# Storing the small inverses of an RWKV-7 recurrence from GpSimd's queue, and two of its last operations on VectorE

## The chip, the core and the metric

The kernel runs on one core of a Trainium2 chip. The metric is the device time of one execution in microseconds (us), lower is better. Engines are named as in the profile: PE is TensorE (matrix products), DVE is VectorE, ACT is ScalarE, POOL is GpSimd, and SP is SyncE, which here does nothing but start transfers. SPq, ACTq and POOLq are the transfer instructions that stand in the instruction stream of SP, ACT and POOL.

## The reference, cut to what matters

One decoder layer over 2048 tokens (plus 16 meta tokens) and 1024 channels: a combined input projection, a sliding-window attention, an RWKV-7 recurrence in parallel with it, a gated merge, an output projection and a SwiGLU network.

```python
proj = u @ w_in[layer] + b_in[layer]
y_attn = sliding_window_sink_attention(q, k, v, attn_sinks[layer])
y_rwkv = rwkv7_time_mix(p_rwkv, ...)
merged = gates[..., :D] * (y_attn @ w_br_attn) + gates[..., D:] * (y_rwkv @ w_br_rwkv)
h = h + merged @ w_o[layer]
h = h + (silu(f @ w_ffn_gate) * (f @ w_ffn_up)) @ w_ffn_down
...
# the recurrence, per head, step by step in time
S = S * w_t + (S @ a_t) b_t + v_t k_t ;  y = S @ r_t
# and its end: group norm of y, then
y = y * ln_w + ln_b
y = y + sum(r * k * r_k) * v          # the bonus
return y * g                          # the output gate
```

## The kernel before

The dense products (input projection `pi`, gated branches `pb`, output projection `ph_o`, network `pg`, `pu`, `ph_d`) run on PE in a fixed program order, block after block of 512 tokens: first phase a for four blocks, then phase c for four blocks. Each 128-row piece of a weight is loaded in float32 by SP (`chunk`, line 212, tile `wr_...`, two buffers), and split by ACT into a high part (`wh_...`) and by DVE into a low part (`wl_...`, five buffers for both); PE uses high and low parts in three products.

Between the dense products the recurrence is woven in. It is cut into 33 units: one for the meta tokens and 32 of 256 tokens and one pair of heads (`rwkv(i, j)`, four chunks of 64 tokens each). Every `yield` of a unit is a place where dense work comes between. The order of PE's instructions is pinned to the order in which the program is written (`InOrder`); the other engines' orders come from a scheduler, and each engine works its own list strictly in turn, so an instruction that waits holds everything behind it on that engine.

In each unit sixteen 32 x 32 triangular matrices are inverted on POOL. PE makes them (`pg`), DVE scales them into `g`, SP stores them to DRAM (`lt_d`, line 744) and loads them back so that each partition has one column to solve for (`lt`, line 754). SP also loads the unit matrix into `xv` (line 757). POOL then does 31 pairs of instructions (lines 761 and 763). The result goes back to DRAM (`xt_d`, line 788) and is loaded as blocks into `td` (line 793), from where the chunk steps (`ch`) use it. `xv` has one buffer: the load of the next unit's `xv` (line 757) must wait until the store of line 788 has read this unit's. `td` has one buffer too.

At a unit's end the chunk outputs are gathered by ACT into `yt` (line 836), normalised, transposed by PE (`pyt`), scaled by ACT into `tl` (line 858), and then the bonus `bv` is added and the gate `gs` multiplied (lines 859 and 860). SP stores the result into `y_d` (line 861), which phase c loads (`yl`, line 415; `ya` is its split).

Of the kernel before, what the change touches and what calls it, by code (L numbers as in the profile page):

```python
# [78 lines left out]
def layer(ctx, tc, x, meta, w_in, w_br, w_o, w_gate, w_up, w_down, w2a, a2, g2, vecs, sinks, gfin,  # L79
          consts, rope, out):  # L80
    nc = tc.nc
    V, A, G, S = nc.vector, nc.scalar, nc.gpsimd, nc.sync
# [43 lines left out]
    xt_d = dp.tile([4 * NU + 1, 16, 32, 32], F32, name="xt_d")  # L126
# [9 lines left out]
    def vc(n, j, rows=slice(None)):  # L136
        return vec[rows, _VC[n][0] + j:_VC[n][0] + j + 1]
# [468 lines left out]
    def rwkv(i, j):  # L606
# [3 lines left out]
        m = i is None  # L610
        uid = 4 * NU if m else 4 * i + j
# [68 lines left out]
        if not m:  # L680
# [10 lines left out]
            gs = t1("gs", 3)  # L691
# [15 lines left out]
        if not m:  # L707
# [3 lines left out]
            bv = t1("bv", 3)  # L711
# [44 lines left out]
        xv = mx.tile([P, 4, 32], F32, tag="xv", bufs=1, name=f"xv_{nm}")  # L756
# [28 lines left out]
                    A.activation(vd[hb, q::2, hb], pvt[qb, :, hb], AF.Copy)  # L785
        for _ in range(WAIT_INV):
            yield
        S.dma_start(xt_d[uid].rearrange("m (b c) i -> b m (c i)", c=4), xv.rearrange("p c i -> p (c i)"))
        lo, hi = [slice(64 * h, 64 * h + 32) for h in range(2)], [slice(64 * h + 32, 64 * h + 64) for h in range(2)]
        for h in range(2):  # L790
            for q, r32 in ((0, lo[h]), (1, hi[h])):
# [64 lines left out]
            T.transpose(pyt[:, t * P:(t + 1) * P], yt[:, t], ident)  # L856
        yf = t1("tl", 2)
        A.activation(yf, pyt[:, :TU], AF.Identity, bias=vc("ln_b", j), scale=vc("ln_w", j))
        G.tensor_add(yf, yf, bv)
        G.tensor_mul(yf, yf, gs)  # L860
        S.dma_start(y_d[4 + j][:, i * TU:(i + 1) * TU], yf)


# [152 lines left out]
    def tick():  # L1016

        turn[0] = (turn[0] + 1) % TURNS
        rs = [u for u in units if u[2] == "r"]
        for u in list(units):  # L1020
            if turn[0] != (0 if u[2] == "a" else 1 if len(rs) > 1 and u is rs[0] else 2):
                continue
            u[1] += 1
            if next(u[0], 0) == 0:
                units.remove(u)
        if todo_r and turn[0] == 2:
            i, j = todo_r[0]
            b = (i or 0) // 2
            young = min((u[1] for u in units if u[2] == "r"), default=LAG)
            if young >= LAG - 3 and i not in asked and set(range(6, 9)) <= emitted[b]:  # L1030
                asked.add(i)
                start("l", lora(i), b)
            if young >= LAG and i in loras and set(
                    range(9, 21) if i is None else range(PAIR0 + 3 * j, PAIR0 + 3 * j + 3)) <= emitted[b]:
                todo_r.pop(0)
                start("r", rwkv(i, j), b)
        if todo_a and turn[0] == 0 and not any(u[2] == "a" for u in units):
            ti = todo_a[0]
            b = (ti or 0) // 4
            if set(range(6)) <= emitted[b]:  # L1040
                todo_a.pop(0)
                start("a", attn_meta() if ti is None else attn(ti), b)
# [135 lines left out]
```

## Time and profile before

| | us |
|---|---|
| three runs: lowest, median, highest | 3446.83, 3450.84, 3458.58 |
| the profiled execution's own time | 3451.51 |
| its span from first to last instruction | 3449.7 |
| mean granted TensorE clock, share of full | 0.976 |

The page of the profile gives the busy time of each engine, and the trace behind it can be asked for single instructions. In all rows times are in microseconds unless marked ns, and L788 is line 788 of the kernel. In a list of waits "A <- B" says that A's engine sat idle until B was done. A transfer instruction's duration is that of its start alone, not of the movement of data.

### The profile page before, as it was taken

The page shows a single profiled execution, that of the slowest core. Times are in us where ns is not written, and L with a number is a line of the kernel's source. Part 1 is how long each engine was busy: PE and PEld are TensorE (multiplying, and loading weights), DVE is VectorE, ACT ScalarE, POOL GpSimd, SP SyncE. Part 2 cuts the span into 40 slices and gives each one's busy share as a digit, 9 for nine tenths or more (in the row PEclk, how much of TensorE's full clock was granted, in tenths as well). Part 3 has the DMA queues.
Part 4 walks back from the last instruction along what each step waited for, and adds up shares of the span by engine and source line. Part 5 has one row for each costly group of instructions (what it writes and reads, how often), then busy time and mean ns, then how long its engine had stood idle before and what let it go on. Part 6 is the DMA issues. An engine that isn't in the chain of part 4 may idle for free.

```text
span 3449.7 us, 47536 instructions
## 1 busy us (share of the span) xinstructions
PE 3285.1 (95%) x16909; PEld 2696.2 (78%) x16909; DVE 1906.8 (55%) x3796; ACT 1499.4 (43%) x3101; POOL 1026.7 (30%) x2321
## 2 busy tenths in 40 slices
PE   8999999999999999999989999999889999999999
PEld 6887777877778777777877788877777888778887
DVE  3344435544444775656666655656665655764555
ACT  4455446555544454445443534434353333432222
POOL 0133333343333344333343334434333332100000
PEclk9999999999999999999999999999999999999999
DMA  4454444454544433333344333324433332532222
GB/s 143 157 145 132 152 127 137 138 154 129 164 129 138 140 103 96 95 96 95 89 142 143 95 94 101 94 85 145 148 94 90 96 91 91 191 98 98 98 97 99
DMA packets 229932, 409.49 MB, mean 119 GB/s; under 512 B 61037, under 2 KB 124013, under 8 KB 229694
## 3 DMA queue, kind: packets, MB, share of 16 engines
q1 hardware_dynamic: 197342, 359.14, 34.4%
q10 hardware_dynamic: 32352, 47.31, 3.9%
q8 instruction: 133, 2.18, 0.3%
q14 instruction: 105, 0.86, 0.1%
HBM read 346.29 MB, written 60.04 MB: 118 GB/s over the span
## 4 chain that ended last, share of the span: by engine, by line
PE 45%; POOL 15%; DMA 7%; issue 7%; DVE 3%; ACT 2%; SPq 1%; POOLq 0%; ACTq 0%; DVEq 0%
PE pg L93 10%; PE pu L93 9%; PE ph_d L93 8%; POOL xv L763 7%; POOL pr L761 7%; PE pi L93 5%; PE pb L93 3%; PE ch L93 2%; DMA lt<-lt_d 2%; PE ph_o L93 2%; PE py L93 1%; DMA lt_d<-g 1%; PE pq L93 1%; DVE h L202 1%; POOL tl L860 1%
## 5 line engine op out<-in xcount | busy, mean ns | idle before, releaser
L93 PE MATMUL pi<-act_u,wh_in 128*128 128x512 f32 x2368 | 765.5, 404 | 2.2 <-DVE act_u L202 2.0
L761 POOL TENSOR_TENSOR pr<-xv,lt 128x124 f32<-128x124 f32 (+30 forms) x992 | 377.6, 381 | 568.2 <-DMA lt<-lt_d 245.4
L93 PEld LDWEIGHTS pi<-act_u,wh_in 128*128 128x128 f32 x2368 | 426.2, 190 | 83.5 <-issue 5.8
L93 PE MATMUL pi<-act_u,wl_in 128*128 128x512 f32 x1184 | 466.8, 394 | 0.4 <-DVE wl_in L202 0.4
L93 PE MATMUL pg<-act_f,wh_g 128*128 128x512 f32 x1408 | 455.0, 404 | 7.0 <-DVE act_f L202 7.0
L93 PE MATMUL pu<-act_f,wh_u 128*128 128x512 f32 x1408 | 449.5, 401 | 0.0
L93 PE MATMUL ph_d<-wh_d,mg_g 128*128 128x512 f32 x1280 | 430.5, 401 | 12.7 <-DVE th L202 10.7
L763 POOL TENSOR_TENSOR xv<-xv,pr 128x124 f32<-128x124 f32 (+30 forms) x992 | 396.5, 400 | 74.2
L93 PEld LDWEIGHTS pg<-act_f,wh_g 128*128 128x128 f32 x1408 | 257.3, 191 | 57.6 <-DVE act_f L202 9.9
L93 PEld LDWEIGHTS pu<-act_f,wh_u 128*128 128x128 f32 x1408 | 259.1, 190 | 50.3 <-issue 1.5
L93 PEld LDWEIGHTS ph_d<-wh_d,mg_g 128*128 128x128 f32 x1280 | 243.3, 190 | 66.3 <-DVE th L202 12.5
L202 DVE TENSOR_TENSOR wl_in<-wr_in,wh_in 128x1024 fp32r<-128x1024 f32 x148 | 186.3, 1259 | 195.7 <-PE pi L93 126.2
L93 PE MATMUL pg<-act_f,wl_g 128*128 128x512 f32 x704 | 278.0, 395 | 0.0
L93 PE MATMUL pu<-act_f,wl_u 128*128 128x512 f32 x704 | 277.1, 394 | 0.0
L93 PEld LDWEIGHTS pi<-act_u,wl_in 128*128 128x128 f32 x1184 | 223.8, 189 | 51.1 <-DVE wl_in L202 0.8
L93 PE MATMUL ph_d<-wl_d,mg_g 128*128 128x512 f32 x640 | 251.9, 394 | 0.0
L850 POOL TENSOR_TENSOR gst<-gst,mhalf 128x4 f32<-128x4 f32 x32 | 35.8, 1119 | 707.5 <-DVE gst L849 610.1
L202 DVE SCALAR_TENSOR_TENSOR h<-ph_d,h 128x512 f32<-128x512 f32 x320 | 216.8, 686 | 52.2 <-PE ph_d L93 51.1
L202 ACT ACTIVATE wh_g<-wr_g 128x1024 fp32r<-128x1024 f32 x88 | 93.3, 1060 | 223.4 <-PE pu L93 72.5
L202 ACT ACTIVATE wh_in<-wr_in 128x1024 fp32r<-128x1024 f32 x148 | 155.8, 1053 | 79.4 <-DMA wr_in<-in_w_in 70.8
L202 DVE TENSOR_TENSOR wl_u<-wr_u,wh_u 128x1024 fp32r<-128x1024 f32 x88 | 109.4, 1243 | 120.4 <-issue 53.9
L202 DVE TENSOR_TENSOR wl_d<-wr_d,wh_d 128x1024 fp32r<-128x1024 f32 x80 | 100.0, 1250 | 129.3 <-PE pg L93 51.2
(356 smaller groups left out, 5965.5 us busy)
## 6 DMA issues: line engine op xcount, KB each, us to landing
wr_in<-in_w_in SPq DMA_DIRECT2D x148, 512.0 KB
wr_g<-in_w_gate SPq DMA_DIRECT2D x88, 512.0 KB
wr_u<-in_w_up SPq DMA_DIRECT2D x88, 512.0 KB
wr_d<-in_w_down SPq DMA_DIRECT2D x80, 512.0 KB
proj_d<-po ACTq DMA_DIRECT2D x84, 256.0 KB
gate_d<-po ACTq DMA_DIRECT2D x64, 256.0 KB
lt<-lt_d SPq DMA_DIRECT2D x32, 512.0 KB
wr_br<-in_w_br SPq DMA_DIRECT2D x32, 512.0 KB
```

Of the source, the lines that this page charges most:

```text
L93: r = f(*p, **k)
L202: return f(*p, **k)
L761: G.tensor_mul(pr[:, :, :n_], xv[:, :, r:r + 1].to_broadcast([P, 4, n_]), lt[:, r, r + 1:].unsqueeze(1).to_broadcast([P, 4, n_]))
L763: G.tensor_add(xv[:, :, r + 1:], xv[:, :, r + 1:], pr[:, :, :n_])
L850: G.tensor_tensor(st[:, 3], st[:, 2], mhalf[:, 0:4], op=ALU.pow)
L860: G.tensor_mul(yf, yf, gs)
```

## The change

The store of each unit's inverses is started by POOL and not by SP, and lines 859 and 860 run on DVE and not on POOL. Nothing else is edited.

```diff
         for _ in range(WAIT_INV):
             yield
-        S.dma_start(xt_d[uid].rearrange("m (b c) i -> b m (c i)", c=4), xv.rearrange("p c i -> p (c i)"))
+        G.dma_start(xt_d[uid].rearrange("m (b c) i -> b m (c i)", c=4), xv.rearrange("p c i -> p (c i)"))
...
         yf = t1("tl", 2)
         A.activation(yf, pyt[:, :TU], AF.Identity, bias=vc("ln_b", j), scale=vc("ln_w", j))
-        G.tensor_add(yf, yf, bv)
-        G.tensor_mul(yf, yf, gs)
+        V.tensor_add(yf, yf, bv)
+        V.tensor_mul(yf, yf, gs)
         S.dma_start(y_d[4 + j][:, i * TU:(i + 1) * TU], yf)
```

The scheduler makes new orders from it. PE's order stays the same. On SP all 33 stores of line 788 are gone. The other transfers keep their order but for seven that moved by one to four places; six of these are loads of the next unit's `xv`, which moved ahead. Three places follow.

SP, around the store of the unit whose inverses are done at 2246.9 us in the trace before (`wr_u` and `wr_g` are weights of the SwiGLU network, `xv_3` is this unit's tile and `xv_0` the next one's):

```order
 L559 DMA rp_1_22717<-proj_d 128x3x257
 L212 DMA wr_g_16_22120<-in_w_gate 128x1024
-L788 DMA xt_d<-xv_3_21635 8x16x128
 L757 DMA xv_0_22373<-in_consts 128x128
 L212 DMA wr_u_16_22193<-in_w_up 128x1024
```

The store left SP's list, and the next unit's `xv` load now follows the load of `wr_g_16` directly. On POOL the same store stands right behind the unit's last addition, ahead of the power of a group norm (line 850) and of the next inverse:

```order
 L761 TENSOR_TENSOR pr_3_30_21727<-xv_3_21635,lt_3_21633 128x4
 L763 TENSOR_TENSOR xv_3_21635<-xv_3_21635,pr_3_30_21727 128x4
+L788 DMA xt_d<-xv_3_21635 8x16x128
 L850 TENSOR_TENSOR gst_2_22274<-gst_2_22274,mhalf 128x4
 L761 TENSOR_TENSOR pr_0_0_22375<-xv_0_22373,lt_0_22371 128x4x31
```

It is the only instruction that POOL gains in a unit.

SP, around the store of the unit whose inverses are done at 2096.6 us (`xv_1` this unit's, `xv_2` the next one's):

```order
 L559 DMA rp_3_21274<-proj_d 128x3x257
 L212 DMA wr_g_9_20654<-in_w_gate 128x1024
-L788 DMA xt_d<-xv_1_20229 8x16x128
+L757 DMA xv_2_20935<-in_consts 128x128
 L212 DMA wr_u_9_20728<-in_w_up 128x1024
-L757 DMA xv_2_20935<-in_consts 128x128
 L212 DMA wr_d_9_0_20777<-in_w_down 128x1024
 L212 DMA wr_d_9_1_20866<-in_w_down 128x1024
```

Here the `xv` load moved ahead of the load of `wr_u_9`.

POOL, at the end of the unit whose `tl` ACT finishes at 1138.6 us (`tl_0`; the inverse that runs at that time is `xv_2`, two units on):

```order
 L761 TENSOR_TENSOR pr_2_5_11136<-xv_2_11119,lt_2_11117 128x4x26
 L763 TENSOR_TENSOR xv_2_11119<-xv_2_11119,pr_2_5_11136 128x4x26
-L859 TENSOR_TENSOR tl_0_11309<-tl_0_11309,bv_0_9350 128x256
 L761 TENSOR_TENSOR pr_2_6_11139<-xv_2_11119,lt_2_11117 128x4x25
-L860 TENSOR_TENSOR tl_0_11309<-tl_0_11309,gs_0_9278 128x256
 L763 TENSOR_TENSOR xv_2_11119<-xv_2_11119,pr_2_6_11139 128x4x25
 L761 TENSOR_TENSOR pr_2_7_11142<-xv_2_11119,lt_2_11117 128x4x24
```

The two instructions stood among the pairs of an inverse and are gone. On DVE they stand among the splits of the branches' inputs (`ya`):

```order
 L783 COPY vd_116<-pvv_2_11326 64x2x64
 L202 TENSOR_TENSOR ya_2_11348<-ye_11293,ya_2_11348 128x512
+L859 TENSOR_TENSOR tl_0_11309<-tl_0_11309,bv_0_9350 128x256
 L202 TENSOR_TENSOR ya_3_11354<-ye_11293,ya_3_11354 128x512
+L860 TENSOR_TENSOR tl_0_11309<-tl_0_11309,gs_0_9278 128x256
 L202 TENSOR_TENSOR ya_4_11376<-ye_11295,ya_4_11376 128x512
 L202 TENSOR_TENSOR wl_br_1_11437<-wr_br_1_11434,wh_br_1_11436 128x1024
```

Each takes a turn between two splits of a block of 512 columns.

## Rows read from the trace of the kernel before

**Rows 1.** The page, busy time and share of the span.

```profile
PE 3285.1 (95%) x16909; PEld 2696.2 (78%) x16909; DVE 1906.8 (55%) x3796; ACT 1499.4 (43%) x3101; POOL 1026.7 (30%) x2321
```

**Rows 2.** Waits of PE: us in total, times, longest.

```profile
PE ch L93 <- ACT yt L836: 41.4, 15, 5.4
```

**Rows 3.** Waits of SP's transfer instructions: us in total, times, longest.

```profile
SPq L788 <- POOL xv L763: 291.2, 28, 14.3
...
SPq L793 <- PE ch L93: 102.0, 24, 9.3
SPq L861 <- POOL tl L860: 100.4, 16, 11.7
...
SPq L757 <- DMA xt_d<-xv: 37.3, 29, 2.2
```

**Rows 4.** Timeline, 2245 to 2255 us: start, duration, instruction, idle before.

```profile
2245.53 1.06 POOL L761 TENSOR_TENSOR pr<-xv,lt 128x4 f32<-128x4 f32 x1
...
2246.67 0.21 POOL L763 TENSOR_TENSOR xv<-xv,pr 128x4 f32<-128x4 f32 x1
...
2246.91 0.60 SPq L788 DMA_DIRECT2D xt_d<-xv  x1
...
2249.07 0.34 SPq L757 DMA_DIRECT2D xv<-in_consts  x1
...
2249.52 0.36 SPq L212 DMA_DIRECT2D wr_u<-in_w_up  x1
...
2253.55 1.06 ACT L202 ACTIVATE wh_u<-wr_u 128x1024 fp32r<-128x1024 f32 x1 [11.45 <-DMA wr_u<-in_w_up]
...
2254.95 0.58 PE L93 MATMUL ch<-vd,g 128*128 128x128 f32 x1 [4.26 <-ACT yt L836]
```

**Rows 5.** Timeline of PE at three other ends of an inverse.

```profile
343.53 1.12 PE L93 MATMUL py<-ptt,vz 128*128 128x512 f32 x2 [3.52 <-ACT ptt L991]
...
2026.13 0.49 PE L93 MATMUL ch<-vd,g 128*128 128x128 f32 x2 [3.00 <-ACT yt L836]
...
2877.92 0.49 PE L93 MATMUL ch<-vd,g 128*128 128x128 f32 x2 [2.24 <-ACT yt L836]
```

**Rows 6.** Timeline of ACT, POOL, SP and PE at two unit ends.

```profile
1138.03 0.55 ACT L858 ACTIVATE tl<-pyt,vec 128x256 f32<-128x256 f32 x1
...
1149.19 0.74 POOL L860 TENSOR_TENSOR tl<-tl,gs 128x256 f32<-128x256 f32 x1
...
1149.96 0.32 SPq L861 DMA_DIRECT2D y_d<-tl  x1
...
1158.35 2.08 PE L93 MATMUL py<-ptt,vz 128*128 128x512 f32 x2 [4.67 <-ACT ptt L991]
...
2379.75 0.80 PE L93 MATMUL ch<-vd,g 128*128 128x128 f32 x2 [5.20 <-ACT yt L836]
```

**Rows 7.** Timeline of ACT after the store at 2096.6 us.

```profile
2100.55 1.06 ACT L202 ACTIVATE wh_u<-wr_u 128x1024 fp32r<-128x1024 f32 x1 [6.17 <-DMA wr_u<-in_w_up]
```

**Rows 8.** Stretches behind PE's stalls: length, busy time by engine (instructions), PEclk, DMA share, GB/s.

```profile
343.50:351.50 8.00, 7.97 (x36) 6.56 (x37) 2.69 (x8) 4.31 (x8) 0.00 (x0) 0.79 0.51 155
1158.40:1166.40 8.00, 8.00 (x26) 5.89 (x27) 6.29 (x11) 5.28 (x11) 6.75 (x17) 0.66 0.66 221
2026.10:2036.10 10.00, 9.97 (x40) 8.69 (x41) 4.81 (x11) 4.72 (x10) 0.00 (x0) 0.66 0.17 52
2379.80:2387.80 8.00, 8.00 (x27) 6.68 (x28) 5.05 (x8) 4.55 (x10) 6.83 (x16) 0.63 0.44 142
...
2877.90:2885.90 8.00, 7.98 (x39) 6.74 (x40) 4.55 (x7) 3.81 (x7) 0.00 (x0) 1.00 0.35 94
```

**Rows 9.** Groups by line and shape on POOL and DVE: busy us, mean ns of one.

```profile
L850 POOL TENSOR_TENSOR gst<-gst,mhalf 128x4 f32<-128x4 f32 x32 | 35.8, 1119 | 707.5 <-DVE gst L849 610.1 <-DMA yl<-y_d 45.6 <-DVE ms L970 31.4
L860 POOL TENSOR_TENSOR tl<-tl,gs 128x256 f32<-128x256 f32 x32 | 28.3, 884 | 0.2
...
L679 DVE TENSOR_TENSOR kp<-kp,rkv 128x256 f32<-128x256 f32 x32 | 13.5, 423 | 0.8
```

## The prediction

> **What bounds the kernel now.** I read the page first: PE is busy for 95% of the span and no other engine for more than 55% [rows 1]. PE's order is pinned, so time can be won only in what PE waits for, some 160 us, and lost only by new waits. The second view is PE's own waits. The largest group is the first product of a chunk step (`ch`), which waits for ACT to copy the previous chunk's output (`yt`) [rows 2]. ACT is busy for 43%, so the question is why it is late. The timeline around such a stall shows it [rows 4]. SP, which works strictly in turn, reached the store L788 and waited for POOL's last addition; the store starts at 2246.91. The next load of `xv` follows at 2249.07, when the store has landed, 2.16 us later. Only then does SP start the load of `wr_u`. ACT, whose next turn is the split of that weight, stands for 11.45 us until 2253.55, copies `yt` behind it, and PE has lost 4.26 us. So a weight queued behind SP's wait for the inverse reaches PE through ACT's turn. The third view, SP's waits, gives the size: 291.2 us in 28 waits of L788 for POOL, about 10 us each; 37.3 us in 29 waits of the `xv` load for the store; and 100.4 us in 16 waits of the store L861 for `tl` from POOL, the second such place [rows 3].
>
> A stall costs PE more than its length. Behind four of the five stalls below, the granted clock of the next 8 or 10 us is 0.63 to 0.79, so a part of the stretch ran at the lower level (1.2 GHz and not 2.4 GHz) after PE had stood idle; behind the one of 2.24 us it is 1.00 [rows 8]. I count length times (1 minus clock) as lost with the stall.
>
> **The change part by part.** The sum is made against the profiled execution's own time, 3451.51, which is 0.7 above the median.
>
> *SP's wait moves, it does not vanish.* L788 leaves SP, but L757 stays there. `xv` has one buffer, so L757 now waits for POOL's store to land, and thereby for the inverse. What is gained lies between the old place of L788 and L757: where a weight load stands there, it no longer waits. Three of PE's stalls are of this kind: 3.52, 3.00 and 2.24 us [rows 5], with clock 8 x 0.21 = 1.7, 10 x 0.34 = 3.4 and 0 [rows 8]. Sum: 8.8 + 5.1 = **13.9 gained**.
>
> *Where nothing stands between,* as at 2246.9 [rows 4], the weight's start depends on when the store lands. I count seven stalls of this kind, like the 4.26 shown. Two things move them. First, the price x of a start by POOL over one by SP, which no row shows. Low end: the same 0.60 [rows 4], x = 0. High end: the store writes 16 rows for each of 8 groups; if POOL needs one shortest instruction, 0.21, for each of the 16, and DVE holds it twice, that is 16 x 0.21 + 2 x 0.85 = 5.1, x = 4.5. (Such a hold is in the rows: an instruction of POOL on 4 elements took 1.06 where its like takes 0.21, so 0.85 more [rows 4].) I take 1.12, the power of L850 [rows 9], POOL's costliest work on few elements, and half a hold, 0.43: 1.55, x = 0.95, nearer to the low end since nearly all rows of POOL on few elements are. Second, L859 and L860 leave the inverse: L860 is 0.88 [rows 9] and L859 a little less, 1.7 together. On DVE they can hold POOL by at most their own length, 2 x 0.42 [rows 9], of which I take half. The inverse is done 1.3 earlier. Net: 0.95 - 1.3 = -0.35 for each of seven, **2.5 gained**; between 9 gained (x = 0) and 22 lost (x = 4.5).
>
> The Trainium skill gives a price for this: "DMA: Bandwidth & Descriptors", section Specifications, has a first byte after about 1 us from GpSimd's queue and after 0.6 from SP's. By the page x would be 0.4, an estimate, and the sum some 5 us less than mine; no row here shows a transfer of POOL's.
>
> *Loads that fell behind L757.* In three units the new order puts loads behind the `xv` load that stood ahead of it: at 2096.6 the load of `wr_u_9`, at 2797.6 one of `wr_d`, at 1762.5 two loads of `y`. They start about 2 us later (the 2.16 of [rows 4], less 0.35). ACT already stands 6.17 us for the first [rows 7], so it is near the path, but PE shows no stall there, so part is slack. I take 2 us for the third, and for the other two half of a stall of 2 us with its clock: **5 lost**; between 0 and 11.
>
> *L859 and L860 on DVE.* 64 instructions of 0.42 us [rows 9] are 27 us, in an engine that is idle 45% of the time [rows 1]. Behind them in DVE's turn stand splits and copies, 0.85 us later in each unit, and longer where ACT's `tl` is not yet done when DVE comes to it. Nearly all of PE's long stalls name ACT, so I take **1 lost**; the high end is 27, if each were on the path.
>
> *SP's second wait.* The store L861 waits until POOL has come to L859 and L860 among the pairs of an inverse. At 1138.58 ACT's part of `tl` was ready, L860 ended at 1149.93, SP's store started at 1149.96, and the weight behind it came so late that PE stood 4.67; in a later unit the same happened with loads of `y`, and PE stood 5.20 [rows 6]. On DVE `tl` is done 0.85 us and one or two instructions of DVE's after ACT, so some 8 us sooner, more than either stall. With clock, 8 x 0.34 = 2.7 and 8 x 0.37 = 3.0 [rows 8], that is 9.9 + 5.7 = **15.6 gained**.
>
> *Given back.* PE then comes earlier to the next place where it depends on an inverse, whose length is fixed by POOL. The two stalls of the last part lie inside the run of an inverse, at whose end SP's wait is then longer. I take a third of 13.9 + 15.6 as given back, **10 lost**; between none and all.
>
> *Nothing* for the `td` loads: they wait for PE's last use of `td` in 24 units [rows 3], so the store has landed long before. If that cover were gone, x would be paid once in a unit by the transposes behind `td`. Nothing for POOL's own time: it is idle 70% of the span [rows 1], and what stands behind the store on its list moves by x less the 1.3.
>
> Sum: -13.9 - 2.5 + 5 + 1 - 15.6 + 10 = -16.0, so 3435.5 for the profiled execution and 3434.8 for the median. I say **3435**, 0.45% faster.
>
> **The rivals.** About 0.3%, 10 us, is what a measurement of this kernel can tell from no change.
>
> *The store holds SP longer (slower).* Ten places depend on x: seven stalls and three moved loads. Each us of x costs 10, so the gain is used up at x = 0.95 + 1.6 = 2.55; from x = 3.6 the time is over the bound, and at 4.5 it is 3435 + 35 = 3470. For it: SP cannot pass L757 before POOL's store lands, and no row bounds POOL's start from above. Against it: POOL's instructions at an inverse's end take 0.21 [rows 4], and its costliest on 4 elements 1.12 [rows 9].
>
> *DVE holds each store (no change).* If DVE holds POOL's start twice in each unit where I took half a hold, x = 0.95 + 1.5 x 0.85 = 2.2, and 10 x 1.27 is lost: 3448. For it: the held row [rows 4], and DVE busy for 55%. The Trainium skill speaks for this: "SBUF — State Buffer", section "A bandwidth-pool intuition that's wrong (but worth ruling out)", tells of a transfer from GpSimd's queue which takes about 0.62 us alone and 3.1 beside a copy on VectorE, since GpSimd could not write its descriptors. By that figure x = 2.5, an estimate, and the time is 3450. The held row agrees that DVE can hold POOL, but for a computation, not for a transfer.
>
> *All is given back (no change).* The way from `lt_d` over `lt`, the inverse and the store to SP is as long as before but for 0.35 us, so PE may gain at the freed places and lose as much at the next inverse: 3435 + 19.5 = 3454. For it: SP's wait at the inverse is 10 us in nearly every unit [rows 3]. Against it: three of the five stalls that go lie at the end of an inverse, farthest from the next.
>
> *More is gained (faster).* With x = 0 at the ten places, 9.5, and nothing given back, 10: 3416. For it: the inverse is done 1.3 earlier, and SP has one instruction less in each unit.
>
> **How the numbers follow.** Forecast 0.40 (its own range 3427 to 3445), longer hold of SP 0.15 (3460 to 3472), hold by DVE 0.13 (3444 to 3456), all given back 0.22 (3444 to 3458), more gained 0.10 (3410 to 3424). Below 3440.5 lie 0.34 of the forecast and the last case: faster 0.44. Above 3461 lie most of the first rival and 0.03 of the third, with an unlucky order on DVE: slower 0.17. Same: 0.39. The range 3420 to 3460 leaves out the first rival and half of the last.
>
> **What the profile after would show.** Right: no wait of SP at L788; waits of L757 of about 10 us each, with POOL's addition or the store as releaser; the waits of L861 down to a third; PE's stalls near 343, 1158, 2026, 2380 and 2878 gone; the one near 2255 still there, within half a us. A POOL row for L788 of 1 to 2 us, and a landing 2.5 to 4 us after the inverse. Wrong: a landing 5 us or more after the inverse (x over 2.5) with longer stalls of `ch`; stalls of PE at new places of about the size of those gone; or DVE named as the releaser of PE behind L859 or L860.

## The result, and the profile after

| | before | changed |
|---|---|---|
| median of the runs, us | 3450.23 | 3420.49 |
| lowest and highest, us | 3446.83 to 3458.58 | 3412.06 to 3430.07 |
| the profiled execution, us | 3451.51 | 3412.06 |
| ratio to before, 95% interval | | 0.991 [0.989, 0.993] |

Timed again beside other kernels, the changed kernel had 3423.8 and a ratio of 0.9918 [0.9905, 0.9932]. The change is worth some 29 us, where 16 were forecast: the sign was right, the size about half.

The page, busy time and share of the span (beside [rows 1]):

```profile
PE 3263.3 (96%) x16909; PEld 2682.7 (79%) x16909; DVE 1929.6 (57%) x3860; ACT 1499.4 (44%) x3101; POOL 1004.8 (29%) x2290
```

DVE has its 64 instructions more and POOL is 22 us less busy. PE's busy time fell by 22 us with the same 16,909 products: less of it ran at the lower clock (the mean granted clock is 0.984, and 0.976 before).

SP's waits (beside [rows 3]) and PE's largest (beside [rows 2]), us in total, times, longest:

```profile
SPq L757 <- DMA xt_d<-xv: 341.5, 30, 17.1
...
SPq L793 <- PE ch L93: 103.6, 25, 9.3
SPq L861 <- DVE tl L860: 46.7, 19, 5.7
SPq L861 <- DVE vd L783: 27.4, 8, 5.6
```

```profile
PE ch L93 <- ACT yt L836: 23.0, 12, 4.9
```

SP's wait did move and not vanish: 291.2 us at L788 and 37.3 at L757 became 341.5 at L757. The waits of L861 fell from 248.6 us (three rows of POOL, of which [rows 3] shows the first) to 78.5, a third row of 4.4 included. PE's wait for `yt` fell by 18.4 us.

Groups by line and shape on POOL and DVE, busy us and mean ns of one (beside [rows 9]):

```profile
L788 POOL DMA_DIRECT2D xt_d<-xv x32 | 21.8, 681 | 9.4 <-POOL xv L763 9.4
```

```profile
L859 DVE TENSOR_TENSOR tl<-tl,bv 128x256 f32<-128x256 f32 x32 | 14.5, 454 | 34.9 <-ACT tl L858 34.7
L860 DVE TENSOR_TENSOR tl<-tl,gs 128x256 f32<-128x256 f32 x32 | 14.4, 450 | 0.6
```

The timeline at the same unit as [rows 4] (start, duration, instruction, idle before):

```profile
2212.61 0.21 POOL L763 TENSOR_TENSOR xv<-xv,pr 128x4 f32<-128x4 f32 x1
2213.12 0.69 POOL L788 DMA_DIRECT2D xt_d<-xv  x1 [0.29 <-POOL xv L763]
...
2215.34 0.33 SPq L757 DMA_DIRECT2D xv<-in_consts  x1
2215.76 0.38 SPq L212 DMA_DIRECT2D wr_u<-in_w_up  x1
...
2219.58 1.06 ACT L202 ACTIVATE wh_u<-wr_u 128x1024 fp32r<-128x1024 f32 x1 [9.17 <-DMA wr_u<-in_w_up]
2220.66 0.27 ACT L836 ACTIVATE yt<-ch 64x128 f32<-64x128 f32 x1
...
2220.99 0.49 PE L93 MATMUL ch<-vd,g 128*128 128x128 f32 x2 [1.98 <-ACT yt L836]
```

Here is what I had not forecast. The chain is the same as in [rows 4], and the `xv` load even comes later behind the inverse, 2.52 us and not 2.19 (over all units the median is 2.70 against 2.20). Yet PE loses 1.98 and not 4.26, because this inverse took 29.5 us and not 31.9. The clock shows the second half of it, in the 8 us behind the places of PE's former stalls near 343, 2026, 2255 and 2878 (length, busy time by engine, PEclk, DMA share, GB/s; beside [rows 8]):

```profile
340.00:348.00 8.00, 7.66 (x43) 6.12 (x42) 2.29 (x7) 3.59 (x7) 0.00 (x0) 1.00 0.63 206
...
2000.00:2008.00 8.00, 8.00 (x47) 6.98 (x47) 4.41 (x12) 4.78 (x10) 0.00 (x0) 1.00 0.35 126
2222.50:2230.50 8.00, 8.00 (x45) 6.87 (x44) 5.70 (x14) 3.52 (x8) 0.00 (x0) 1.00 0.25 73
...
2840.00:2848.00 8.00, 8.00 (x40) 6.71 (x39) 3.61 (x6) 2.54 (x5) 0.00 (x0) 1.00 0.32 91
```

All of it at 2.4 GHz. Before, the 8 us behind the stall at 2255 had 0.72, and [rows 8] has the others:

```profile
2255.00:2263.00 8.00, 8.00 (x36) 7.02 (x37) 3.96 (x10) 3.34 (x9) 0.00 (x0) 0.72 0.19 66
```

At 2255 the shorter stall returned its 2.3 us and the stretch at the lower clock as well.

And here is where the gain of L861 went. Timeline after the unit's end near 1138 us of [rows 6]:

```profile
1144.87 0.32 SPq L451 DMA_DIRECT2D tg<-gate_d  x1
...
1157.43 0.68 POOL L788 DMA_DIRECT2D xt_d<-xv  x1 [0.29 <-POOL xv L763]
...
1159.86 0.33 SPq L757 DMA_DIRECT2D xv<-in_consts  x1
1160.28 0.38 SPq L212 DMA_DIRECT2D wr_br<-in_w_br  x1
...
1164.28 1.06 ACT L202 ACTIVATE wh_br<-wr_br 128x1024 fp32r<-128x1024 f32 x1 [7.97 <-DMA wr_br<-in_w_br]
...
1165.89 0.69 DVE L202 TENSOR_TENSOR mg_m<-mt,mg_m 128x512 fp32r<-128x512 f32 x1 [6.60 <-ACT mg_m L202]
...
1167.49 0.79 PE L93 MATMUL ph_o<-wh_o,mg_m 128*128 128x512 f32 x1 [5.01 <-DVE h L202]
```

The stall of 4.67 us is gone, and SP, whose last start before was at 1144.87, now stands 15 us at L757 for the running inverse. A weight of the branches waits behind it, its split on ACT comes late, DVE waits for ACT, and PE loses 5.01 us.

**The forecast's terms in the traces.** PE does the same products in the same order in every kernel here, so its lead over the kernel before can be read at any product: the product's start in one trace less its start in the other. The gain over a stretch is the change of that lead, the stall and the stretch at the lower clock together. Two profiles of the changed kernel (3412.06 and 3430.8 us, the fastest and the slowest of its eight timed executions) give, with a minus for what was gained:

| term | forecast | first | second |
|---|---|---|---|
| three stalls with loads between L788 and L757 | -13.9 | -13.7 | -13.5 |
| seven stalls with nothing between | -2.5 | -13.3 | -9.1 |
| loads that fell behind L757, three units | +5 | +3.3 | +4.0 |
| L861, two stalls | -15.6 | -14.6 | -14.9 |
| given back (measured: at the next stall behind those two) | +10 | +13.8 | +15.6 |
| everything else (forecast: DVE) | +1 | -15.1 | -3.1 |
| sum | -16.0 | -39.6 | -20.8 |

### The profile page after: what moved, and what is told of

Its sections match the earlier page's. It is cut to its first block, busy times and chain, and to the rows that moved or that the text cites. A ratio compares the mean times of both kernels' runs of the same rounds, so it can differ in the third digit from the quotient of the medians.

```text
span 3410.3 us, 47506 instructions
## 1 busy us (share of the span) xinstructions
PE 3263.3 (96%) x16909; PEld 2682.7 (79%) x16909; DVE 1929.6 (57%) x3860; ACT 1499.4 (44%) x3101; POOL 1004.8 (29%) x2290
## 4 chain that ended last, share of the span: by engine, by line
PE 46%; issue 20%; POOL 20%; DMA 7%; DVE 4%; ACT 2%; SPq 1%; POOLq 0%; ACTq 0%; DVEq 0%
PE pi L93 15%; POOL pr L761 9%; POOL xv L763 8%; PE pg L93 7%; PE pu L93 7%; PE ph_d L93 5%; PE ch L93 2%; PE pb L93 1%; PE ph_o L93 1%; PE py L93 1%; DMA lt<-lt_d 1%; DMA wr_in<-in_w_in 1%; DMA xt_d<-xv 1%; DVE h L202 1%; PE ph_d_l L93 1%
## 5 line engine op out<-in xcount | busy, mean ns | idle before, releaser
L761 POOL TENSOR_TENSOR pr<-xv,lt 128x124 f32<-128x124 f32 (+30 forms) x992 | 398.1, 401 | 584.6 <-DMA lt<-lt_d 468.9
L763 POOL TENSOR_TENSOR xv<-xv,pr 128x124 f32<-128x124 f32 (+30 forms) x992 | 380.9, 384 | 76.5
```

Of the source, the lines that this page charges most:

```text
L761: G.tensor_mul(pr[:, :, :n_], xv[:, :, r:r + 1].to_broadcast([P, 4, n_]), lt[:, r, r + 1:].unsqueeze(1).to_broadcast([P, 4, n_]))
L763: G.tensor_add(xv[:, :, r + 1:], xv[:, :, r + 1:], pr[:, :, :n_])
```

## The experiments

Two theories at the start. A: the gain is SP's, since weight loads no longer stand behind its wait at L788. B: the gain is POOL's, since inverses without L859 and L860 end earlier, and every wait that hangs on their end shortens. In the later runs B says it more sharply: the end of an inverse reaches PE through SP's wait for it and no other way. The twelve kernels were timed in three groups of four, with "before" beside each: 3448.89, 3450.75 and 3452.59 us. A difference between kernels of two groups is good to some 4 us.

**Each half alone.** The store on POOL, the rest as before:

```diff
-        S.dma_start(xt_d[uid].rearrange(...), xv.rearrange(...))
+        G.dma_start(xt_d[uid].rearrange(...), xv.rearrange(...))
```

> The store L788 is started by POOL as in the change, L859 and L860 stay on POOL. Theory A (the gain is SP's: weight loads no longer stand behind SP's wait at L788): most of the 30 us are here, so 3430 or less; the PE stalls near 340, 2023 and 2876 of the kernel before are gone, together about 13 us. Theory B (the gain is POOL's: with L859 and L860 gone each inverse and all that waits for it is done 1 to 3 us earlier): the same three stalls are gone, but the moved loads cost 4 us and the store's landing, 0.5 us later than by SP in the two profiles, costs about 6 with its clock at the seven places, so 3443 to 3450; the stalls near 1356, 2174 and 2251 stay at 3.7 us or more.

Measured 3433.99, ratio 0.9949 [0.9932, 0.9967], 15 us faster: between the two. The three stalls returned 13.5 us, none of it given back. The seven lost 0.7 in all, although the landing is 0.5 us later in each (median 2.69).

L859 and L860 on DVE, the store on SP:

```diff
-        G.tensor_add(yf, yf, bv)
-        G.tensor_mul(yf, yf, gs)
+        V.tensor_add(yf, yf, bv)
+        V.tensor_mul(yf, yf, gs)
```

> L859 and L860 run on DVE as in the change, SP starts the store L788 as before. Theory A: only the store L861 is freed, and the two stalls that this frees come back at the next inverse, as in the two profiles, so 3445 to 3450. Theory B: the inverses are as short as in the changed kernel, the stalls near 1356, 2174 and 2251 of before shrink by about 2 us each and lose their stretch at the lower clock, so 3425 to 3434, more than half of the 30 us; the three stalls near 340, 2023 and 2876 shrink by 1 to 2 us but stay.

Measured 3443.56, ratio 0.9977 [0.9966, 0.9989], 5 us faster, nearest to A's range. The inverses are as short as in the changed kernel (mean 29.6 us), but by the lead the two stalls of L861 gained 14.1 and lost 15.5 right behind, and the seven gained 2.6 only, a new stall of 6.3 us near 2232 among them; another of 5.7 us came near 2713. At both a load of `wr_g` that stood ahead of L788 before now stands between L788 and L757. The scheduler's new order put it there, and by the lead the two stalls cost 7.9 and 7.8 us. B in its first form falls short: shorter inverses did not bring most of the gain while the store stood on SP. Part of that is the new order, so this run does not give their price alone; without the first of the new stalls the seven gained 10.6. Together the halves bring more, 29 us, than the sum of both, 20, and the two new stalls, which the store on POOL removes, are enough for that difference.

**The inverse longer and shorter.** In the changed kernel, four idle additions in each inverse:

```diff
+            if r == 15:
+                for _ in range(4):
+                    G.tensor_add(pr, cst[:, :P]..., cst[:, :P]...)
```

> The changed kernel with four idle additions of 128x128 on POOL in the middle of each inverse, about 0.4 us each, so that each inverse is some 1.8 us longer and SP's and DVE's parts of the change stay; the output is the same. Theory A: no more than 4 us slower than the changed kernel, 3424. Theory B: what the shorter inverses gave comes back, 14 to 20 us, 3434 to 3441, with the stalls near 1356, 2174 and 2251 again at about 4 us.

Measured 3457.01, ratio 1.0026 [1.0012, 1.0039]: 33 to 37 us slower than the changed kernel (3423.8 and 3420.49), more than either theory had, and slower than the kernel before. The mean inverse went from 29.94 to 32.36 us, 2.4 and not the 1.8 expected, so 14 to 15 us for each of them. The unit of [rows 4] again (lines behind the additions count three more):

```profile
2249.12 0.33 SPq L757 DMA_DIRECT2D xv<-in_consts  x1
2249.54 0.38 SPq L212 DMA_DIRECT2D wr_u<-in_w_up  x1
...
2253.76 1.06 ACT L202 ACTIVATE wh_u<-wr_u 128x1024 fp32r<-128x1024 f32 x1 [12.70 <-DMA wr_u<-in_w_up]
...
2255.16 0.80 PE L93 MATMUL ch<-vd,g 128*128 128x128 f32 x2 [5.55 <-ACT yt L839]
```

The stall is 5.55 us. In 8 us that begin 0.8 behind that product the clock is 0.81 (from the product on, 2255.20 to 2263.20, it is 0.76):

```profile
2256.00:2264.00 8.00, 8.00 (x40) 6.93 (x40) 4.49 (x12) 3.33 (x8) 0.00 (x0) 0.81 0.18 66
```

The other direction, the last four pairs left out (part of the solution is not computed):

```diff
-        for r in range(31):
+        for r in range(27):
```

> The changed kernel without the last four of the 31 pairs of each inverse (part of the solution is left out), so each inverse is some 2.3 us shorter and nothing else is touched. With longer inverses the changed kernel lost 36 us for 2.4 us, 15 per us. Theory B (the end of the inverse sets the stalls at a steady price, through SP): 20 to 35 us faster than the changed kernel, 3386 to 3400. Theory A (the places that the end of an inverse could free are used up, and only longer ones cost): 3412 or more.

Measured 3399.46, ratio 0.9859 [0.9842, 0.9876]: 21 to 24 us faster than the changed kernel for 2.9 us less (mean 27.03), so 7 to 8 per us, in B's range.

**The load of `xv` on POOL's queue as well,** in the changed kernel:

```diff
-        S.dma_start(xv.rearrange("p c i -> p (c i)"), consts[...])
+        G.dma_start(xv.rearrange("p c i -> p (c i)"), consts[...])
```

> The changed kernel with the load of xv, L757, also started by POOL, so that SP waits neither for the inverse nor for its store. Theory A (SP's turn is what makes the stalls at an inverse's end): the stalls that are left there in the changed kernel (near 1344, 1498, 1847, 2147, 2242, 2451 and 2616, together 25 us and some 17 of the lower clock) go, less a third given back: 3385 to 3397. Theory B (the inverse itself is late, whoever starts the transfers): the transposes behind td need it as before and stalls come back at other places, so a gain of 10 us or less, 3410 to 3420.

Measured 3358.67, ratio 0.9743 [0.9725, 0.9762]: 62 to 65 us faster than the changed kernel, beyond A's range and far from B's. Theory B as that run had it, that the inverse is late whoever starts the transfers, fails here; what is left of B is that the inverse's end counts through SP. By the lead over the kernel before, the seven stalls have now returned 48.2 us, of which the changed kernel had 9 to 13, and the long stall near 1760 us, which loads of `y` ended, another 12. The same unit:

```profile
2179.13 0.69 POOL L788 DMA_DIRECT2D xt_d<-xv  x1 [0.29 <-POOL xv L763]
...
2179.51 1.06 ACT L202 ACTIVATE wh_u<-wr_u 128x1024 fp32r<-128x1024 f32 x1 [3.39 <-PE ph_d L93]
...
2181.40 0.28 ACT L836 ACTIVATE yt<-ch 64x128 f32<-64x128 f32 x1 [0.83 <-DVE sd L834]
2181.58 0.57 POOL L757 DMA_DIRECT2D xv<-in_consts  x1 [1.76 <-DMA xt_d<-xv]
...
2184.55 0.38 PE L93 MATMUL ch<-vd,g 128*128 128x128 f32 x2
```

The wait for the store stands on POOL, where it holds nothing up. ACT does not wait for the weight but for PE, and `ch` has no stall.

Does the inverse's length still matter then? The same kernel with the four idle additions:

> The changed kernel with the load of xv on POOL, and with the four idle additions in each inverse, some 2.4 us longer. Theory B (an inverse's length costs PE through SP's wait for it, and by no other way): within 8 us of the same kernel without the additions, 3355 to 3367. Rival (the way over xt_d and td to the chunk steps sets PE's stalls itself, or POOL's other work behind the inverse does): 25 to 40 us slower than that, 3384 to 3398.

Measured 3364.41, ratio 0.9760 [0.9742, 0.9777]: 6 us slower, with intervals that overlap, where the same additions cost 33 to 37 with the load on SP (mean inverse 29.83 and 32.43 us). This shows B in its sharper form: some five sixths of what an inverse's length costs went through SP's wait.

**The load of `xv` on POOL's queue and nothing else,** against the kernel before:

> The kernel before with the load of xv, L757, started by POOL; the store stays on SP and L859 and L860 on POOL. SP still stands at L788 until the inverse is done, 290 us in all, but no longer until the store has landed, 37 us. Theory B (each us that SP's turn comes later behind an inverse costs 15): 2.2 us less behind each inverse, about 30 us faster than before, 3415 to 3425. Theory A (weights that stood between the store and the load are not helped, and the rest comes back later): 3436 or more.

Measured 3430.92, ratio 0.9945 [0.9926, 0.9964]: 20 us faster, between the theories. SP is free 2.2 us earlier behind each inverse, 9 us per us; in a profiled execution 8 us under the median the seven returned 21.3, and the three nothing (they lost 1.3), since their loads stay behind L788.

**Both transfers on POOL's queue, L859 and L860 still on POOL:**

> The kernel before with both the store L788 and the load L757 started by POOL; L859 and L860 stay on POOL. SP then waits for POOL at L861 alone, some 245 us. Theory B (any wait of SP for POOL's inverse reaches PE through the weights behind it): 20 us or more slower than the kernel with L859 and L860 on DVE, 3380 to 3400. Theory A (once L788 and L757 are off SP, L861 has slack, since its two stalls came back elsewhere): within 8 us of it, 3355 to 3367.

Measured 3377.37, ratio 0.9794 [0.9777, 0.9811]: 18.7 us slower than with L859 and L860 on DVE, a little under B's range. So the second half of the change is worth 19 us once SP does not stand at L757, and 5 where it stands at L788.

**What DVE pays.** The changed kernel without L859 and L860 (bonus and gate not computed):

> The changed kernel without L859 and L860 (the bonus and the gate are left out), so DVE has 64 instructions fewer and tl goes to the store as ACT leaves it. If these instructions are hidden on DVE, as the prediction has it with 1 us: within 5 us of the changed kernel, 3415 to 3425. If they are on the path through the splits behind them: 10 us or more faster, 3410 or less.

Measured 3418.22, ratio 0.9900 [0.9887, 0.9914], against 3423.8 beside it: 5.6 us, with intervals that overlap, and within the range for hidden instructions. Nothing like 27. The changed kernel itself in the same group:

> The changed kernel as it is, timed again beside the others: 3420, between 3414 and 3426.

Measured 3423.8, ratio 0.9918 [0.9905, 0.9932], as expected.

**SP without its wait for `tl`:** in the kernel with both transfers on POOL and the two instructions on DVE, the store L861 on ACT's queue.

```diff
-        S.dma_start(y_d[4 + j][:, i * TU:(i + 1) * TU], yf)
+        A.dma_start(y_d[4 + j][:, i * TU:(i + 1) * TU], yf)
```

> The changed kernel with the load of xv on POOL, and the store L861 started by ACT, so that SP also stands no longer for tl, 68 us in its waits. Theory B (any wait on SP for an engine's result costs PE through the weights behind it): 5 to 15 us faster than the kernel with the load of xv on POOL alone, 3343 to 3354. Rival (ACT, which then waits for DVE's two instructions behind L858, 0.85 us or more in each of 32 units, passes it on to PE): no gain or slower, 3357 to 3375.

Measured 3362.13, ratio 0.9734 [0.9721, 0.9748]: no gain, as the rival had it. In the kernel without this edit SP's waits at L861 are at most 5.4 us long. Whether they had slack, or ACT, which now stands for DVE's two instructions, lost what SP won, this run does not tell apart.

**The early place of the load alone.** In the changed kernel the load of `xv` stays on SP, but is kept behind the load of `lt` in SP's order (`late` keeps an instruction where the program writes it):

```diff
-        S.dma_start(xv.rearrange("p c i -> p (c i)"), consts[...])
+        late(S.dma_start(xv.rearrange("p c i -> p (c i)"), consts[...]))
```

> The changed kernel with the load of xv still on SP, but kept behind the load of lt in SP's order, where the store has landed long before. Theory B (what is left of SP's wait for the inverse is only the early place of this load): as fast as with the load on POOL, 3352 to 3364, and no wait at L757. Rival (POOL's queue was what helped, or the load of xv then comes late for the next inverse): 3375 or more.

Measured 3349.0 (3341.84 to 3349.91), ratio 0.9694 [0.9681, 0.9707]: the fastest of all, 104 us under before and 3 under B's range. SP's waits have no row of L757 or L788 any more:

```profile
SPq L744 <- DVE g L745: 121.3, 32, 11.2
SPq L793 <- PE ch L93: 102.3, 25, 7.2
SPq L861 <- DVE tl L860: 44.6, 20, 5.2
SPq L861 <- DVE vd L783: 28.8, 9, 6.6
SPq L793 <- DMA xt_d<-xv_None: 13.5, 1, 13.5
```

SP now starts it beside the load that the next inverse needs anyway, when the store has long landed:

```profile
2134.33 1.75 SPq L744 DMA_DIRECT2D lt_d<-g  x4
2137.25 0.60 SPq L754 DMA_DIRECT2D lt<-lt_d  x1
2137.90 0.45 SPq L757 DMA_DIRECT2D xv<-in_consts  x1
```

## Why the prediction was half right

**"SP's wait moves, it does not vanish"** held, and so did its term: 13.9 forecast, 13.5 to 13.7 in both profiles and in the store alone. All of it stays.

**"Where nothing stands between" is the step that failed.** I forecast 2.5 us for the seven stalls, and 9 to 13 came, at or beyond my bound of 9 for x = 0; the stall near 2255, which was to stay within half a us, fell from 4.26 to 1.98. The mechanism was right and its size was not: three of its numbers were off the same way. The price x was 0.5 and not 0.95: POOL's start takes 0.68 us, not 1.55, and the landing came 0.5 later in the median; 0.27 of that passes between POOL's last addition and the start. By the two first-byte figures of the Trainium skill ("DMA: Bandwidth & Descriptors", section Specifications) x is 0.4, an estimate, and the 0.5 of the trace is near it. Second, the inverses of these seven units got shorter by 1.4 and 1.6 us in the mean of the two profiles, three of them by 2.2 to 2.9, where I had 1.3. The net is then 0.9 to 1.15 us for each and not 0.35. Third, I counted a us of stall as a us, though I had priced the clock at the other places: 4.26 to 1.98 was worth 4.4 by the lead. I had seen the stretch at the lower clock behind long stalls and did not ask what becomes of it when a stall only shrinks.

**Small stalls were put at nothing.** My sum has no term for PE's other stalls, most of them under 2 us. "Everything else", where I had +1 for DVE alone, came to -15.1 and -3.1: in the mean of the two profiles a miss about as large as that of the seven.

**"Loads that fell behind L757"** was right in size: 5 forecast, 3.3 and 4.0.

**"SP's second wait" and "given back"**: the gain of L861 was right, 15.6 forecast and 14.6 to 14.9 measured, but the third that I took as given back, spread over all gains, was the wrong split. The freed loads at an inverse's end gave nothing back; the two stalls inside the run of an inverse gave all back within some 30 us, at new places (1167 and 2364) and about in their own size, the first at L757 (the timeline at 1160). That this was the place is shown by the kernel with `xv` on POOL, where the first return is 0.0. The second return is another wait, "Nothing for POOL's own time" in my working: a power of the final norm (L232) stands on POOL behind the inverse and the store.

```profile
2360.29 0.69 POOL L788 DMA_DIRECT2D xt_d<-xv  x1 [0.30 <-POOL xv L763]
2361.00 0.58 POOL L232 TENSOR_TENSOR ss_o<-ss_o,mhalf 128x1 f32<-128x1 f32 x1
2361.61 0.72 ACT L202 ACTIVATE h<-h,ss_o 128x512 f32<-128x512 f32 x1 [6.83 <-POOL ss_o L232]
2361.61 0.75 DVE L202 SCALAR_TENSOR_TENSOR h<-h,ss_o,gft 128x512 f32<-128x512 f32 x1 [6.28 <-POOL ss_o L232]
...
2364.53 0.79 PE L93 MATMUL ph_d_l<-wh_d_l,mg_g 128*128 128x512 f32 x1 [5.13 <-DVE h L202]
```

POOL idle for 70% of the span is no cover for an instruction that stands behind a 30 us run; with `xv` on POOL 5.5 us of this return remain.

**"L859 and L860 on DVE"**, 1 us: no more than about 6 by the kernel without them, so hidden for the most part.

**What stays open.** The cause of "everything else", 15 and 3 us in the two profiles. It is made of some thirty steps of 0.4 to 4 us, gains and losses. A part comes back in both profiles: at eleven stalls of 0.2 to 1.5 us before (near 519, 601, 681, 845, 857, 1074, 1323, 1441, 1619, 2307 and 2709) the lead grew by 11.0 and 9.7 us in all, and at one of 2.0 us near 2983 by 2.9. What differs between the two executions are the other steps. I did not try them one by one.

**The rivals.** The store did not hold SP for long and no hold by DVE shows: of the 32 loads of `xv` behind a store 30 start 2.5 to 3.5 us behind the inverse, the first two at 4.3 to 4.4, and L788 takes 0.65 to 0.81 us in all units. Of the 33 stores 30 landed 2.1 to 2.4 us after their start, whether DVE stood idle meanwhile or worked for up to 2.7 us. The 3.1 us that the Trainium skill ("SBUF — State Buffer", section "A bandwidth-pool intuition that's wrong (but worth ruling out)") gives is for such a transfer beside a copy on VectorE. Beside these 33 stores DVE ran 0.2 us of copies in all, so this case does not test that figure. "All is given back" was true of one half only. "More is gained" came nearest in time, 3416, but by luck: x was not 0, and 14 to 16 us were given back.

## What to carry to other kernels

Moving an in-order queue's wait to another instruction of the same queue frees only what stood between the two. Before costing such a move, ask what the next instruction of that queue waits for: here one more line, a load kept later in the same queue, was worth two and a half times the change itself. And price a stall by PE's lead at the same product in two traces, with the stretch at the lower clock behind it, since a stall that shrinks from 4 us to 2 can return more than those 2.

## What the runs showed of the hardware

- POOL's start of this transfer (8 groups of 16 rows) took 0.68 us in the mean, SP's 0.60 [rows 4], and the landing came 0.5 us later in the median. The whole price of the other queue was half a us in a unit.
- The stretch at the lower clock behind a stall is not in proportion to it: in the 8 us that begin at the same product the granted clock was 1.00 after a stall of 1.98 us, 0.72 after one of 4.26 us and 0.76 after one of 5.55 us. The seven stalls of before, 32 us long in all by their rows, were worth 48 us when all but 0.7 of them was gone (the load of `xv` on POOL).
- Two executions of the changed kernel that differ by 18.7 us (3412.06 and 3430.8) agree within 0.3 us on the three freed stalls, and differ by 4 on the seven and by 12 on all small stalls together: most of the spread between these two sits in short stalls.
